# A block of mLSTM and sparse attention on one core: 256 bytes between two families of tiles, and the bias rows stored once

## The chip, the cores and the metric

The kernel runs on one core of one Trainium2 chip. The metric is device time in microseconds; less is better. The core has TensorE (matmuls), VectorE, ScalarE, POOL (GpSimd) and SP (SyncE); SP and POOL issue the transfers, which share 16 DMA engines.

## The reference

One layer on 256 tokens of width 4096, all in float32:

```
h = rmsnorm(x) * norm_w
u = h @ w_in                       # 4096 x 15424, split into 16 parts
y_ml = mlstm(conv/silu(q, k), v, gates), normed per head, * sigmoid(o) * silu(z)
y_ns = nsa(q, compressed, selected and window keys/values, rel_bias) * silu(z)
x = x + concat(y_ml, y_ns) @ w_out               # 4096 x 4096
x = x + sigmoid(x @ ple_gate) * (p @ ple_proj)   # 4096 x 4096, 256 x 4096
```

In `nsa` each score gets a bias that depends on the head and, through 32 buckets, on the distance of query and key: `bias = rel_bias[bucket(t - s)]`, with s > t masked. With 256 tokens all blocks are selected and the window holds all of them, so that selected and window branch differ in their keys and values only.

## The kernel before, in words

**The wide matmuls.** A float32 product is made of three float32r products. An operand `a` is split into `a_hi`, its rounded copy, and `a_lo = a - a_hi`; the result is `hi*hi + hi*lo + lo*hi`. The activations are the stationary operands: 8 tiles `sh0` to `sh7` (high parts) and 8 `sl0` to `sl7` (low parts), each 128 partitions x 4 x 256, 4096 bytes in a partition, filled for the first phase by `split_x` and for the later two by `t_stat`. The weights stream as the moving operand: a unit is a 512 KB block of 256 rows x 512 columns, loaded by SP into one of five `raw` buffers, split by ScalarE (`whi`, line 983) and VectorE (`wlo`, line 984) into one of three buffers each, two units ahead (`LOOK = 2`), and used in 12 matmuls (`mm` in `wide_group`, lines 725 to 735): for each of two row blocks j, `whi` with `sh` for both token halves t, `whi` with `sl` for both, `wlo` with `sh` for both. 16 units make a group of 512 output columns. There are 30 groups for `w_in`, 8 for `w_out` and 8 for `ple_gate`, and between them units of other kinds: 4 for the small columns of `w_in` (`small_group`, where the roles of weights and activations are exchanged), 16 for the compression and 8 for `ple_proj` (`proj_unit`, lines 885 to 897, with the stationary tiles `ph` and `pl`).

**Order.** The program's order is written out: the main loop at the end of `hymba_block` issues for each unit the split of the unit two ahead, the next load, the unit's matmuls, and then one `step()` of a queue of generators that hold all other work (`t_nq`, `t_mlstm` and so on). Each engine works in that order.

**The bias.** `t_tables` makes the row `p0[head, i]` by a matmul of the table with a one-hot matrix (`_onehot`), copies it to `rext` (16 x 384) and stores it to `rext_d` in device memory, 128 copies for each head (line 189). In `t_nq`, once for each of four head groups, `load_tb(h)` fetches for each head a tile `tb` of 128 x 256 (line 407): partition p reads 256 values from the p-th copy, shifted by p, so that row p of `tb` holds the bias of query p against keys in rising order. `bias_max` adds it to the scores in PSUM (line 471), for both branches at once. `tb` has three buffers, shared with `mb` of the mLSTM, whose 128 partitions all read the same 1 KB row of `mrow_d` (`load_m`, line 574).

**Where tiles lie.** A pool places its tags one behind another in the order in which they are first used, each tag with all its buffers. In the pool `wk` that order is `u` (3 buffers), `raw` (5 x 4096 bytes in a partition), `whi` and `wlo` (3 x 4096 each), then `sh0`, `sl0`, `sh1`, `sl1` and so on, among them `nat0` to `nat3` (8192 each; they also hold `kh` and `kl`), then `qt` (2 x 4096; `qh` and `ql`), `s` (3 x 2048), `sq` (4096), `b` (8320; also `vsw` and `pl`), `pt` (2 x 2048), `tb` (3 x 1024) and `a` (8320; also `ph`). So before the change `raw`, `whi`, `wlo`, all `sh` and `sl`, `nat`, `qt` and `b` start at the same place within 512 bytes, and `a` 128 bytes further on (8320 is 16 x 512 + 128).

Of the kernel before, what the change touches and what calls it, by code (L numbers as in the profile page):

```python
# [11 lines left out]
F32 = mybir.dt.float32  # L12
# [32 lines left out]
def hymba_block(ctx: ExitStack, tc: tile.TileContext, a, out: bass.AP):  # L45
    nc = tc.nc
# [5 lines left out]
    wk = ctx.enter_context(tc.tile_pool(name="work", bufs=1))  # L52
    psp = ctx.enter_context(tc.tile_pool(name="psum", bufs=1, space=bass.MemoryType.PSUM))
    drp = ctx.enter_context(tc.tile_pool(name="dram", bufs=1, space=bass.MemoryType.DRAM))
    ctx.enter_context(tc.manual_schedule())

    def side(i, shape):
        return psp.tile(shape, F32, tag=f"sd{i}", name=f"sd{i}")
# [4 lines left out]
    def sqtile(shape):  # L63
        return wk.tile(shape, F32, tag="sq", name="sq")

    def stile(shape):
        return wk.tile(shape, F32, tag="s", name="s", bufs=3)
# [4 lines left out]
    def small(shape, tag, bufs=2):  # L72
        return sm_.tile(shape, F32, tag=tag, name=tag, bufs=bufs)
# [47 lines left out]
    hss = cp.tile([128, 2, 8], F32, name="hss")  # L121
    rr = cp.tile([128, 2, 8], F32, name="rr")
    mrow_d = drp.tile([8, 256], F32, name="mrow_d")
    rext_d = drp.tile([16, 128, 384], F32, name="rext_d")


    fifo, urgent = deque(), deque()
# [45 lines left out]
    def t_tables():  # L173
        oh = sqtile([33, 864])
        nc.gpsimd.dma_start(oh, a["onehot"])
        for _ in range(4):
            yield
        p0 = side(0, [16, 384])
        MM(p0, rel33, oh[:, 0:384], start=True, stop=True)
        p1 = side(1, [128, 15, 16])  # L180
        for c in range(15):

            i0 = 384 + 128 - 16 * c - 31 + 255
            MM(p1[:, c, :], oh[:, i0:i0 + 128], rel33, start=True, stop=True)
            if c % 5 == 4:
                yield
        rext = stile([16, 384])
        nc.vector.tensor_copy(rext, p0)
        nc.gpsimd.dma_start(rext_d, rext[:, None, :].to_broadcast([16, 128, 384]))
        nc.vector.tensor_copy(biasc[:, 0:15], p1)  # L190
        yield

# [195 lines left out]
    def t_nq(flag, g):  # L388
# [14 lines left out]
        tb = {}  # L403

        def load_tb(h):
            tb[h] = wk.tile([128, 256], F32, tag="tb", name="tb", bufs=3)
            nc.gpsimd.dma_start(tb[h], bass.AP(tensor=rext_d.tensor,  # L407
                                               offset=rext_d.offset + (4 * g + h) * 128 * 384 + 127,
                                               ap=[[383, 128], [1, 256]]))

        for h in range(2):
            load_tb(h)
# [42 lines left out]
        def scores(i):  # L455
            h, t = units[i]
            n = 128 * (t + 1)
            psd[i] = side(0, [128, 2, n])
            r = slice(t * 128, (t + 1) * 128)
            MM(psd[i], qh[:, h, r], kh[:, g, :, 0:n], start=True, stop=False)  # L460
            MM(psd[i], ql[:, h, r], kh[:, g, :, 0:n], start=False, stop=False)  # L461
            MM(psd[i], qh[:, h, r], kl[:, g, :, 0:n], start=False, stop=True)  # L462
            if t == 0 and h + 2 < 4:
                load_tb(h + 2)

        def bias_max(i):
            h, t = units[i]
            n = 128 * (t + 1)
            sb[i] = stile([128, 2, n])
            bias = tb[h] if t else tb[h][:, 128:256]  # L470
            nc.vector.tensor_tensor(sb[i], psd[i], bias[:, None, :].to_broadcast([128, 2, n]), op=OP.add)  # L471
            mx[i] = small([128, 2], "mx2", 3)
            nc.vector.tensor_reduce(mx[i], sb[i], axis=AX.X, op=OP.max, negate=True)  # L473
# [41 lines left out]
        for i in range(11):  # L515
            at(scores, i)
            at(scale, i - 2)
            at(expo, i - 1)
            at(copy_pt, i - 3)
            yield  # L520
            at(coef, i - 1)
            at(bias_max, i)
            at(trans, i - 2)
            at(pv, i - 3)
            yield
# [123 lines left out]
    sh, sl = [None] * 8, [None] * 8  # L649

    def new_stat(c):
        sh[c] = wk.tile([128, 4, 256], F32R, tag=f"sh{c}", name=f"sh{c}")
        sl[c] = wk.tile([128, 4, 256], F32R, tag=f"sl{c}", name=f"sl{c}")

# [98 lines left out]
    def add(*gens):  # L753
        fifo.extend(gens)
# [4 lines left out]
    def split_x(k):  # L759
        c, kk = divmod(k, 4)  # L760
        if kk == 0:
            new_stat(c)
        x = xraw[c][:, kk]
        nc.scalar.activation(sh[c][:, kk], x, AF.Copy, scale=nw[:, k:k + 1])  # L764
        nc.vector.scalar_tensor_tensor(sl[c][:, kk], x, nw[:, k:k + 1], sh[c][:, kk],  # L765
                                       op0=OP.mult, op1=OP.subtract)

    def p1_post(name):
# [3 lines left out]
        def post(ps, flag):  # L772
# [4 lines left out]
            elif name in ("ks", "kw"):  # L777
                add(t_k(ps, flag, int(name == "kw")))
                if name == "kw":
                    add(t_tables())  # L780
            elif name in ("vs", "vw"):
                add(t_v(ps, flag, int(name == "vw")))
            elif kind == "nz":
                urgent.append(t_nz(ps, flag, i))
            elif kind == "nq":
                urgent.append(t_evac(ps, flag))
                add(t_nq(flag, i))
            elif kind in ("mq", "mk"):
                urgent.append(t_evac(ps, flag))
                add(t_mqk(flag, int(kind == "mk"), i))  # L790
            elif kind == "mv":
                urgent.append(t_mv(ps, flag, i))
                if i == 3:
                    add(t_mlstm(1))
            elif kind == "mz":
                add(t_mz(ps, flag, i))
                if i == 1:
                    add(t_mlstm(0))
            elif kind == "mo":
                add(t_mo(ps, flag, i))  # L800
                ch = [(c, (c * 512 + 2048) % 4096, f"p1_{c}", f"y{c}") for c in range(8)]
                if i == 2:
                    add(t_stat(ch[:7], range(16)))
                if i == 3:
                    add(t_stat(ch[7:], range(16)))
# [81 lines left out]
    def proj_unit(n):  # L887
        def mm(hi, lo):
            ps = [side(2 * (n % 2) + t, [128, 512]) for t in range(2)]
            ph, pl = held["ph"], held["pl"]  # L890
            for t in range(2):
                tk = slice(t * 128, (t + 1) * 128)
                for j in range(2):
                    MM(ps[t], ph[:, j, tk], hi[:, j, :], start=(j == 0), stop=False)  # L894
                    MM(ps[t], pl[:, j, tk], hi[:, j, :], start=False, stop=False)  # L895
                    MM(ps[t], ph[:, j, tk], lo[:, j, :], start=False, stop=(j == 1))  # L896
            pbox[n] = ps
        gemm_unit(a["ple_proj"][n], mm, (lambda: require("r7")) if n == 0 else None)
# [12 lines left out]
    def t_out(ps, flag, n):  # L911
        u = utile([128, 2, 512])
        if n == 7:
            for t in range(2):
                for c in (slice(0, 256), slice(256, 512)):
                    nc.scalar.activation(u[:, t, c], ps[t][:, c], AF.Sigmoid)
                    nc.vector.tensor_tensor(u[:, t, c], u[:, t, c], pbox[n][t][:, c], op=OP.mult)
                    nc.vector.tensor_add(u[:, t, c], u[:, t, c], nat[3][:, t, 512 + c.start:512 + c.stop])
                nc.sync.dma_start(out[t * 128:(t + 1) * 128, n * 512:(n + 1) * 512], u[:, t])
            done.add(flag)  # L920
            return
        for t in range(2):
            nc.scalar.activation(u[:, t], ps[t], AF.Sigmoid)
        done.add(flag)
        yield
        for t in range(2):
            nc.vector.tensor_tensor(u[:, t], u[:, t], pbox[n][t], op=OP.mult)
            nc.vector.tensor_add(u[:, t], u[:, t], nat[n // 2][:, t, (n % 2) * 512:(n % 2) * 512 + 512])
            nc.gpsimd.dma_start(out[t * 128:(t + 1) * 128, n * 512:(n + 1) * 512], u[:, t])
            yield  # L930

    for n in range(8):
        wide_group(f"g{n}", a["ple_gate"][n], "r" if n == 0 else None,
                   lambda ps, flag, n=n: add(t_out(ps, flag, n)), after=lambda u, n=n: proj_unit(n) if u == 7 else None)
# [86 lines left out]
def _bucket(dist):  # L1021
    n = np.maximum(dist, 0)
    nf = np.maximum(n, 1).astype(np.float32)
    large = 16 + (np.log(nf / np.float32(16)) / np.float32(np.log(8.0)) * np.float32(16)).astype(np.int32)
    return np.where(n < 16, n, np.minimum(large, 31))


def _onehot():
    d = np.concatenate([255 - np.arange(384), np.arange(480) - 255])
    o = np.zeros((33, d.size), np.float32)  # L1030
    o[np.where(d < 0, 32, _bucket(d)), np.arange(d.size)] = 1.0
    return o
# [63 lines left out]
```

## Time and profile before

| | |
|---|---|
| Median of 3 runs | 2208.91 us (2208.33 to 2209.18) |
| Profiled execution | 2208.36 us, its span 2206.6 us |
| Mean granted TensorE clock | 0.998 of full |
| TensorE busy | 2190.5 us, 99% of the span |
| VectorE, ScalarE busy | 1155.1 and 993.9 us, 52% and 45% |
| Moved by DMA | 425.14 MB, mean 193 GB/s |

The span goes from the first to the last instruction; the profiled execution's time holds 1.76 us around it. Busy times are unions of an engine's instructions; a matmul's recorded end is modelled, since matmuls overlap in the engine, so that the distance of starts tells the pace. Idle time of an engine that is not the bottleneck costs nothing.

### The profile page before, as it was taken

The numbers are of one execution on the slowest core, as the hardware profiler recorded it, in microseconds if no ns is written. First come the engines' busy times: TensorE is split into PE (matmuls) and PEld (weight loads), VectorE is DVE, ScalarE is ACT, GpSimd is POOL, SyncE is SP. The second block draws the span as 40 slices with busy tenths as digits, with TensorE's granted clock in tenths as the row PEclk, the third lists the DMA queues.
The fourth block names the chain that finished last, engine by engine and source line by source line (L and its number), as shares of the span: only waits on it lengthen the run. The fifth ranks groups of instructions, "written<-read, shape, count | busy, mean of one in ns | idle before, by whom it ended". The sixth has DMA issues, their size and how long they took to land.

```text
span 2206.6 us, 26113 instructions
## 1 busy us (share of the span) xinstructions
PE 2190.5 (99%) x10020; PEld 1800.3 (82%) x10020; DVE 1155.1 (52%) x1361; ACT 993.9 (45%) x1235; POOL 38.7 (2%) x82
## 2 busy tenths in 40 slices
PE   9999998999999999999999999999999999999998
PEld 7876886888888888888888888888888888888887
DVE  6553553555555565744574445564444455544544
ACT  6543443454545455444454344453333344444443
POOL 1000000000000000000000000000000000000000
PEclk9999999999999999999999999999999999999999
DMA  9667568655545454665556665656666655666664
GB/s 356 206 199 262 187 191 174 206 170 165 167 158 179 155 171 147 181 199 185 179 188 196 195 185 175 205 188 206 203 210 205 196 175 186 203 211 201 204 204 134
DMA packets 118796, 425.14 MB, mean 193 GB/s; under 512 B 13794, under 2 KB 13834, under 8 KB 118672
## 3 DMA queue, kind: packets, MB, share of 16 engines
q1 hardware_dynamic: 113840, 408.47, 58.3%
q0 software_dynamic: 4688, 15.00, 3.0%
q8 instruction: 78, 1.28, 0.2%
q14 instruction: 46, 0.38, 0.0%
q10 hardware_dynamic: 144, 0.02, 0.0%
HBM read 416.08 MB, written 7.35 MB: 192 GB/s over the span
## 4 chain that ended last, share of the span: by engine, by line
PE 98%; DMA 1%; DVE 0%; ACT 0%; SPq 0%; issue 0%; ACTq 0%
PE mm L733 60%; PE mm L735 30%; DMA raw<-in_w_in 1%; PE sd L508 1%; PE sd L843 1%; PE sd L663 1%; PE sd L504 1%; PE sd L495 0%; PE sd L203 0%; PE sd L894 0%; PE sd L896 0%; PE sd L895 0%; PE sd L418 0%; PE sd L462 0%; PE sd L461 0%; PE sd L460 0%
## 5 line engine op out<-in xcount | busy, mean ns | idle before, releaser
L984 DVE TENSOR_TENSOR wlo<-raw,whi 128x1024 fp32r<-128x1024 f32 x743 | 910.3, 1225 | 990.0 <-ACT whi L983 981.1
L983 ACT ACTIVATE whi<-raw 128x1024 fp32r<-128x1024 f32 x743 | 787.5, 1060 | 1108.0 <-PE mm L733 986.5
L733 PE MATMUL mm<-whi,sh 128*128 128x512 f32 x2940 | 920.0, 394 | 7.6 <-ACT whi L983 7.6
L733 PE MATMUL mm<-whi,sl 128*128 128x512 f32 x2940 | 908.4, 390 | 0.0
L735 PE MATMUL mm<-wlo,sh 128*128 128x512 f32 x2940 | 907.6, 390 | 0.2
L735 PEld LDWEIGHTS mm<-wlo,sh 128*128 128x128 f32 x2940 | 552.4, 188 | 117.4 <-DVE wlo L984 1.5
L733 PEld LDWEIGHTS mm<-whi,sl 128*128 128x128 f32 x2940 | 552.7, 188 | 116.6
L733 PEld LDWEIGHTS mm<-whi,sh 128*128 128x128 f32 x2940 | 543.7, 188 | 121.2 <-ACT whi L983 10.5
L508 PE MATMUL sd<-vsw,pt 128*128 128x128 f32 x192 | 29.9, 292 | 0.0
L478 ACT ACTIVATE s<-s,mx 128x128 f32<-128x128 f32 (+1 forms) x64 | 28.2, 442 | 0.4 <-DVE mx L473 0.4
L508 PEld LDWEIGHTS sd<-vsw,pt 128*128 128x128 f32 x192 | 23.8, 191 | 3.9
L488 ACT ACTIVATE s<-s,sm 128x128 f32<-128x128 f32 (+1 forms) x64 | 25.2, 441 | 0.4 <-DVE sm L484 0.3
L547 DVE SCALAR_TENSOR_TENSOR sq<-u,convw_c,sq 128x256 f32<-128x256 f32 x48 | 23.3, 485 | 1.7
L152 ACT ACTIVATE u<-mm,rt 128x512 f32<-128x512 f32 x12 | 8.2, 687 | 25.4 <-PE mm L735 25.4
L473 DVE TENSOR_REDUCE mx<-s 128x2 f32<-128x256 f32 (+1 forms) x32 | 17.7, 553 | 1.1
L471 DVE TENSOR_TENSOR s<-sd,tb 128x256 f32<-128x256 f32 (+1 forms) x32 | 17.7, 553 | 0.0
L500 DVE COPY pt<-sd 128x256 f32<-128x256 f32 (+1 forms) x32 | 17.6, 551 | 0.0
L843 PE MATMUL sd<-raw,xq 128*60 128x256 f32 x128 | 17.3, 391 | 0.0
L407 POOL DMA_DIRECT2D tb<-rext_d x16 | 8.6, 537 | 469.4 <-DVE s L471 405.4
L154 DVE TENSOR_SCALAR u<-mm,rt 128x512 f32<-128x512 f32 x12 | 9.0, 751 | 14.5 <-PE mm L735 14.5
L495 PEld LDWEIGHTS sd<-idn,s 128*128 128x128 f32 x96 | 12.4, 140 | 4.2
L765 DVE SCALAR_TENSOR_TENSOR sl<-u,nw,sh 128x256 fp32r<-128x256 f32 x32 | 14.1, 481 | 3.1 <-ACT sh L764 3.0
(223 smaller groups left out, 704.0 us busy)
## 6 DMA issues: line engine op xcount, KB each, us to landing
raw<-in_w_in SPq DMA_DIRECT2D x479, 512.0 KB, 3.5
raw<-in_w_out SPq DMA_DIRECT2D x128, 512.0 KB, 3.5
raw<-in_ple_gate SPq DMA_DIRECT2D x128, 512.0 KB, 4.1
raw<-in_w SPq DMA_DIRECT2D x16, 512.0 KB, 3.5
u<-in_xt SPq DMA_DIRECT2D x16, 256.0 KB, 7.8
xn<-in_x SPq DMA_DIRECT2D x4, 1024.0 KB, 6.7
u<-in_x POOLq DMA_DIRECT2D x8, 512.0 KB, 4.2
raw<-in_ple_proj SPq DMA_DIRECT2D x8, 512.0 KB, 3.8
```

The lines of the kernel that those rows point to most:

```text
L471: nc.vector.tensor_tensor(sb[i], psd[i], bias[:, None, :].to_broadcast([128, 2, n]), op=OP.add)
L478: nc.scalar.activation(sb[i][:, b], sb[i][:, b], AF.Exp, bias=mx[i][:, b:b + 1], accum_out=sums[i][:, b:b + 1])
L488: nc.scalar.activation(sb[i][:, b], sb[i][:, b], AF.Copy, scale=sums[i][:, b:b + 1])
L504: MM(o[t][:, h, :], pct[32 * h:32 * h + NCMP, t, :], vcmp[32 * h:32 * h + NCMP, g, :], start=True, stop=False)
L508: MM(o[t][:, h, :], ptb[i][:, b, s, :], v[:, s, b, g * 128:(g + 1) * 128], start=False, stop=(b == 1 and s == t))
L547: nc.vector.scalar_tensor_tensor(acc[:, h], c[:, h, i:i + 256], w[:, i:i + 1], acc[:, h], op0=OP.mult, op1=OP.add)
L663: nc.tensor.transpose(pp[i // 2][:, i % 2, t * 128:(t + 1) * 128], src[:, t, k:k + 128], idn)
L733: MM(box["ps"][t], s[c][:, k, t * 128:(t + 1) * 128], m[:, j, :], start=st, stop=False)
L735: MM(box["ps"][t], sh[c][:, k, t * 128:(t + 1) * 128], lo[:, j, :], start=False, stop=last)
L843: MM(o[64 * kv:64 * kv + 60], xq[l // 8][:, l % 8, 60 * kv:60 * kv + 60], raw[:, j, 256 * kv:256 * kv + 256], start=(l == 0), stop=(l == 31))
L983: nc.scalar.activation(hi, r, AF.Copy)
L984: nc.vector.tensor_sub(lo, r, hi)
```

## The change

Two things are changed that do not touch each other.

First, a tile `gap` of 128 x 64 float32 (256 bytes in a partition), which nothing writes or reads, is asked for just before `sh0`. All tags that come behind it in the pool `wk` start 256 bytes later; `u`, `raw`, `whi` and `wlo` stay where they were.

Second, the bias row is stored once for each head (16 x 384 in place of 16 x 128 x 384), and in rising order of distance. Partition p of `tb` then reads the 256 values that start at p + 1 of that one row, which puts the keys in falling order, and `bias_max` reads the tile backwards.

```diff
@@ hymba_block
-    rext_d = drp.tile([16, 128, 384], F32, name="rext_d")
+    rext_d = drp.tile([16, 384], F32, name="rext_d")
@@ t_tables
         nc.vector.tensor_copy(rext, p0)
-        nc.gpsimd.dma_start(rext_d, rext[:, None, :].to_broadcast([16, 128, 384]))
+        nc.gpsimd.dma_start(rext_d, rext)
@@ load_tb
             nc.gpsimd.dma_start(tb[h], bass.AP(tensor=rext_d.tensor,
-                                               offset=rext_d.offset + (4 * g + h) * 128 * 384 + 127,
-                                               ap=[[383, 128], [1, 256]]))
+                                               offset=rext_d.offset + (4 * g + h) * 384 + 1,
+                                               ap=[[1, 128], [1, 256]]))
@@ bias_max
-            bias = tb[h] if t else tb[h][:, 128:256]
+            bias = tb[h][:, n - 1::-1] if n == 256 else tb[h][:, 127::-1]
@@ new_stat
     def new_stat(c):
+        if c == 0 and sh[0] is None:
+            wk.tile([128, 64], F32, name="gap")
         sh[c] = wk.tile([128, 4, 256], F32R, tag=f"sh{c}", name=f"sh{c}")
         sl[c] = wk.tile([128, 4, 256], F32R, tag=f"sl{c}", name=f"sl{c}")
@@ _onehot
-    d = np.concatenate([255 - np.arange(384), np.arange(480) - 255])
+    d = np.concatenate([np.arange(384) - 128, np.arange(480) - 255])
```

## Rows read from the trace of the kernel before

**Rows 1.** The page's busy us of each engine, share of the span, instructions.

```profile
PE 2190.5 (99%) x10020; PEld 1800.3 (82%) x10020; DVE 1155.1 (52%) x1361; ACT 993.9 (45%) x1235; POOL 38.7 (2%) x82
```

**Rows 2.** From the page, the chain that ended last, by engine and by line.

```profile
PE 98%; DMA 1%; DVE 0%; ACT 0%; SPq 0%; issue 0%; ACTq 0%
PE mm L733 60%; PE mm L735 30%; DMA raw<-in_w_in 1%; PE sd L508 1%; PE sd L843 1%; PE sd L663 1%; PE sd L504 1%; PE sd L495 0%; PE sd L203 0%; PE sd L894 0%; PE sd L896 0%; PE sd L895 0%; PE sd L418 0%; PE sd L462 0%; PE sd L461 0%; PE sd L460 0%
```

**Rows 3.** The page's groups: busy us, mean ns of one, idle before.

```profile
L735 PE MATMUL mm<-wlo,sh 128*128 128x512 f32 x2940 | 907.6, 390 | 0.2
```

**Rows 4.** Timeline of TensorE, 1600 to 1611 us: start, us, instruction, count.

```profile
1601.14 0.62 PE L733 MATMUL mm<-whi,sh 128*128 128x512 f32 x2
...
1610.66 0.62 PE L733 MATMUL mm<-whi,sh 128*128 128x512 f32 x2
```

**Rows 5.** DMA issues: queue, count, KB each, median us to landing.

```profile
rext_d<-s POOLq DMA_DIRECT2D x1, 3072.0 KB, 35.4
tb<-rext_d POOLq DMA_DIRECT2D x16, 128.0 KB, 3.3
...
mb<-mrow_d POOLq DMA_DIRECT2D x8, 128.0 KB, 4.9
```

**Rows 6.** Timeline of POOL, 340 to 390 us, idle time before.

```profile
381.95 1.08 POOL L407 DMA_DIRECT2D tb<-rext_d  x2 [34.60 <-DMA rext_d<-s]
```

**Rows 7.** Stretch, length; busy PE, PEld, DVE, ACT, POOL; clock, DMA share, GB/s.

```profile
355.00:366.70 11.70, 11.70 (x53) 9.49 (x51) 3.68 (x3) 2.40 (x3) 0.00 (x0) 1.00 0.97 119
...
372.40:379.30 6.90, 5.49 (x12) 3.81 (x12) 1.23 (x1) 1.06 (x2) 0.00 (x0) 0.59 1.00 177
379.30:386.50 7.20, 6.47 (x24) 4.39 (x25) 4.34 (x4) 3.44 (x5) 1.86 (x4) 1.00 1.00 382
```

**Rows 8.** Timeline of 366 to 387 us, TensorE and ScalarE.

```profile
366.24 0.61 PE L735 MATMUL mm<-wlo,sh 128*128 128x512 f32 x2
371.35 1.06 ACT L983 ACTIVATE whi<-raw 128x1024 fp32r<-128x1024 f32 x1 [12.01 <-DMA raw<-in_w_in]
...
372.46 1.22 PE L733 MATMUL mm<-whi,sh 128*128 128x512 f32 x2 [5.61 <-ACT whi L983]
...
386.51 0.61 PE L733 MATMUL mm<-whi,sh 128*128 128x512 f32 x2
```

**Rows 9.** Instructions that touch tb: ns min/median/max, first and last start.

```profile
L471 DVE TENSOR_TENSOR s<-sd,tb x32: 417/554/687, 448.6 to 866.2; 128x256 f32<-128x256 f32 x16, 128x512 f32<-128x512 f32 x16
```

**Rows 10.** Groups by shape, line 471 on VectorE: busy us, mean ns.

```profile
L471 DVE TENSOR_TENSOR s<-sd,tb 128x512 f32<-128x512 f32 x16 | 10.9, 684 | 0.0
L471 DVE TENSOR_TENSOR s<-sd,tb 128x256 f32<-128x256 f32 x16 | 6.8, 423 | 0.0
```

**Rows 11.** Busy us of each engine in the first attention group's stretch.

```profile
420.00:540.00 120.00, 120.00 (x578) 98.97 (x578) 66.59 (x97) 60.80 (x98) 2.46 (x5) 1.00 0.54 167
```

**Rows 12.** Line 735, ns min/median/max: 366.7-372 us, then 1600-1700.

```profile
L735 PE MATMUL mm<-wlo,sh x1: 388/388/388, 366.5 to 366.5; 128*128 128x512 f32 x1
...
L735 PE MATMUL mm<-wlo,sh x147: 388/389/390, 1600.7 to 1700.0; 128*128 128x512 f32 x147
```

**Rows 13.** Timeline of TensorE about the first projection unit, 1851 to 1855 us.

```profile
1851.73 0.40 PE L894 MATMUL sd<-whi,ph 128*128 128x512 f32 x1
...
1854.54 0.63 PE L733 MATMUL mm<-whi,sh 128*128 128x512 f32 x2
```

**Rows 14.** Line 895 over the span: ns min/median/max.

```profile
L895 PE MATMUL sd<-whi,pl x32: 393/397/398, 1852.0 to 2178.6; 128*128 128x512 f32 x32
```

**Rows 15.** Timeline of TensorE about a score, 452 to 454 us.

```profile
452.46 0.39 PE L460 MATMUL sd<-kh,qh 128*128 128x512 f32 x1
...
453.14 0.62 PE L733 MATMUL mm<-whi,sh 128*128 128x512 f32 x2
```

**Rows 16.** Timeline of TensorE in the mLSTM, 1031 to 1033 us.

```profile
1031.23 0.60 PE L601 MATMUL sd<-mv,pt 128*128 128x257 f32 x2
...
1032.10 0.60 PE L603 MATMUL sd<-mv,pt 128*128 128x257 f32 x2
```

## The prediction

> **What bounds the kernel now.** I read the page's first line of engines, then the chain that ended last, then the groups of instructions, and only then single stretches. TensorE is busy for 2190.5 of 2206.6 us, VectorE and ScalarE for about half [rows 1], and the chain is TensorE for 98%, 90% of it the three-product matmuls of lines 733 and 735 [rows 2]. So two things can change the time: the pace of those matmuls, and the places where TensorE stands still. There are 46 wide groups of 16 units of 12 matmuls, 8832 in all (the groups show 2940 of each of three kinds [rows 3]; 12 more, the last unit's, are written out at line 722). Their pace is read from starts, since ends are modelled: from 1601.14 to 1610.66 us lie 42 matmuls, 226.7 ns each, 2.72 us a unit [rows 4]. 512 columns at the 2.4 GHz level are 213.3 ns, so 13.3 ns of each matmul is something else. The one item in the chain that is not TensorE is a weight load from memory, 1% [rows 2]; it is a single stop, and the change reaches it.
>
> **The stop at 367 us.** The DMA list has one large entry that is no weight: the copy of the bias rows, 3072 KB, 35.4 us to landing [rows 5]. The first tb load on POOL waits for it for 34.60 us and goes out at 381.95 [rows 6], so it ran from about 346. Between 355 and 379 us the 16 DMA engines are full, yet move 119 to 177 GB/s; about its landing they move 382 [rows 7]. The weight loads share these engines, and the ring of five raw tiles runs dry. The last pair of a unit starts at 366.24, so the next unit was due at 366.69; it starts at 372.46, two more follow late, and the fourth starts at 386.51 [rows 8]. ScalarE's split ahead of it had waited 12.01 us for raw, not for TensorE [rows 8], so the data was late. Part of the loss is the clock: TensorE stood still, and in the stretch from 372.40 the granted clock is 0.59 of full, so mostly the 1.2 GHz level [rows 7]. In all, 386.51 - 366.69 = 19.82 us for three units that take 8.16: 11.66 us lost, after which the pace is the old one.
>
> **The change, part by part.**
>
> *The row copy.* 3072 KB become 24 KB (16 rows of 1.5 KB), still one DMA on POOL's queue. The stop goes if its cause goes; bounds are 0 (another cause) and 11.66 us. I take 11.66, because the DMA engines are full in just this stretch and before it the loads kept up. POOL's wait of 34.60 us for the landing [rows 6] shrinks to a few us; behind it on POOL stand the tb loads and the clearing of sc, and nothing else late waits for those: the first tb load went out at 381.95 and is first read at 448.6 [rows 6, 9].
>
> *The tb loads.* As before 16 loads of 128 KB, but the 128 partitions now read overlapping stretches of the same 1.5 KB. The nearest row is mb, where all partitions read one 1 KB row: 4.9 us against 3.3 [rows 5]. So 0 to 1.6 us more for each, 25.6 us of transfer at most. Hidden: two loads are issued at a head-group's start, and the rest when heads 0 and 1 are done with a buffer, two heads ahead of their use; in 448.6 to 866.2 us 16 heads are worked [rows 9], so some 26 us for each. Without that cover it would be 1.6 us times 16 on the path.
>
> *The reversed read.* 32 additions on VectorE, 684 and 423 ns at the two shapes [rows 10], now step backwards through tb. No row shows such a read. Bounds: no difference, or doubled, 16 x (0.684 + 0.423) = 17.7 us in all. I take none: the nearest rows are these instructions themselves, and shapes, types and the PSUM operand stay as they are. Its cover: VectorE is busy for 66.6 of 120 us in a head-group's stretch [rows 11], and 4.4 us more for its four heads fit beside that; with the cover gone it would be the 17.7 us.
>
> *The gap.* It lies behind whi and wlo, so the split weights stay where they are and every sh and sl tile moves by 256 bytes. Tags lie in order of first use, and all these tiles are 4096 bytes (or 8192), with slices at multiples of 512. So before, every stationary slice has the same place within 512 bytes as the moving tile beside it; after, it is 256 bytes off. What is this worth? TensorE loads the next stationary slice while the present matmul streams. One matmul had no load beside it, the last before the stop, because the next load waited for the split: 388 ns, against a median of 389 with a load beside it [rows 12]. It is one sample of a modelled end, but the matmuls that are slow by their starts are long by this measure too (below). So in step, the load costs 1 to 2 ns, and the 13.3 ns is nearly all the matmul's own and out of the gap's reach. Bounds: the group mean of 390 ns for a kind without waits [rows 3], less 388, times 8832, is 17.7 us of gain at most. On the other side stand the projection's matmuls. Their stationary tiles ph and pl lie in tags a and b, and ph is 128 bytes off whi within 512, pl is not: 12 of them take from 1851.73 to 1854.54, 234.2 ns each, and the median is 397 instead of 389 [rows 13, 14]. That is 7.5 ns worse, times 8832 = 66 us. The scores, whose tiles moved with each other and lie at one place within 512, hold the old pace right after wide matmuls: three from 452.46 to 453.14 [rows 15], 226.7 ns each. I take 0 between -17.7 and +66: in the projection the offset changes from one matmul to the next, while behind the gap it is one and the same for all, as it is now.
>
> The Trainium skill, in "SBUF — State Buffer", section "Who interferes with whom", gives TensorE two independent read ports, one for the moving operand and one for weight loads. By that rule an address could not matter and the gap is worth 0. The projection's row, at 234.2 ns, disagrees with it; the matmul without a load, at 388 ns, nearly agrees.
>
> *Sum.* The profiled execution took 2208.36 us, its span 2206.6 and 1.76 around it. 2208.36 - 11.66 + 0 + 0 = 2196.70. The median of the runs lies 0.55 above the profiled one, so 2197.2; I forecast **2197 us**, 0.53% faster.
>
> **Rivals.**
>
> *The gap takes away what the load still costs.* For: that cost is seen, 1 to 2 ns [rows 3, 12]. Against: an offset of 256 bytes stands in no row. Time: 2197 less 0 to 17.7, so 2179 to 2195, the middle 2188.
>
> *Slower: the gap puts the loads out of step.* The mechanism is the projection's, in all 8832 matmuls. It decides from 11.66 us / 8832 = 1.3 ns per matmul; the full price gives 2263. For: the only row with another offset is slower. Against: it is a mixture of offsets.
>
> *The 13.3 ns are a collision after all, and the gap takes it away.* Matmuls that read at half the rate (257 columns in the time of 512) carry little: four from 1031.23 to 1032.10, 217.5 ns each, against 214.2 for their columns [rows 16], an excess of 3.3. If the wide ones came down to this, 10 ns x 8832 = 88 us: 2109. Against it speaks the 388 ns of the matmul with nothing beside it. The Trainium skill, "TensorE: Matmul & The Clock Gate", section "Wait — 56ns, not 53.3ns?", gives 2.5 ns of fixed cost per matmul and 215.7 ns for 512 columns; by that the wide matmuls have some 11 ns to lose, 97 us, an estimate from that page. The trace's 226.7 ns disagrees with it for this data type.
>
> *The stop stays.* If 128 partitions that read one row hold up the weight loads, or the stop has another cause, the time is 2208. Against: eight mb loads do the same, and the chain names no stop there [rows 2, 5].
>
> **How the numbers follow.** Forecast as summed 0.50; the load's cost goes 0.25; out of step 0.15; the collision 0.04; the stop stays 0.06. The first two and the stop that stays lie in 2179 to 2212 and hold 0.81; upwards that includes a loss of 1.7 ns per matmul on top of the stop's gain. The forecast's own range is 2193 to 2200. About 0.2%, 4.4 us, is what a measurement of this kernel can tell from no change. Faster by more: 0.50 + 0.25 + 0.04 and a little of the stop that stays, 0.81. Slower by more: 0.14 of the out of step case. The rest, 0.05, within.
>
> **What would show it.** Right: the chain has no weight load of 25 us, TensorE is busy throughout 355 to 395 us, rext_d is 24 KB and lands in a few us; line 471 stays at 684 and 423 ns; tb lands in 3 to 5 us; starts of wide matmuls stay 226.7 ns apart, median 389. Wrong: starts 225 apart or less (the first rival), 228 or more (the second), 217 (the third), or ScalarE waiting for raw about 370 us (the last).

## The result, and the profile after

The changed kernel takes 2197.34 us (median of 4 runs, 2196.65 to 2197.64), the kernel before 2208.62 us on the same chip (4 runs, 2207.94 to 2209.18): a ratio of 0.9949, 95% interval 0.9931 to 0.9966. The forecast was 2197 us. The profiled execution took 2197.64 us, its span 2195.9. One run of e9_shift below took 3590.20 us at a granted clock of 0.571, and its figures are those of the other three.

The page of the changed kernel: busy us of each engine with share and instructions, and the chain that ended last.

```profile
PE 2187.6 (100%) x10020; PEld 1799.3 (82%) x10020; DVE 1154.4 (53%) x1361; ACT 994.0 (45%) x1235; POOL 38.2 (2%) x82
...
PE 100%; DVE 0%; ACT 0%; ACTq 0%; issue 0%
```

Beside [rows 1, 2] the chain has lost its only item of 1% or more that was not TensorE, the weight load. The groups of matmuls (busy us, mean ns of one, idle before) have not moved by more than 1 ns; the third row answers to [rows 3]. Two line numbers more come from the lines of the gap.

```profile
L735 PE MATMUL mm<-whi,sh 128*128 128x512 f32 x2940 | 918.8, 394 | 0.0
L735 PE MATMUL mm<-whi,sl 128*128 128x512 f32 x2940 | 906.6, 390 | 0.0
L737 PE MATMUL mm<-wlo,sh 128*128 128x512 f32 x2940 | 905.8, 389 | 0.0
```

The stretches about the old stop, with the columns of [rows 7]:

```profile
355.00:366.70 11.70, 11.70 (x53) 9.71 (x52) 5.79 (x5) 5.52 (x6) 0.00 (x0) 1.00 0.67 200
366.70:372.40 5.70, 5.70 (x27) 4.73 (x26) 2.71 (x3) 2.12 (x2) 0.00 (x0) 1.00 0.67 215
372.40:379.30 6.90, 6.90 (x32) 5.69 (x32) 2.52 (x3) 3.11 (x3) 0.00 (x0) 1.00 0.60 178
379.30:395.00 15.70, 15.70 (x71) 13.01 (x70) 7.35 (x6) 5.75 (x7) 0.00 (x0) 1.00 0.59 195
```

TensorE is busy throughout, the clock is at its upper level, and up to 379 us the DMA engines are at 0.60 to 0.67 instead of full, while they move 178 to 215 GB/s instead of 119 to 177. The timeline of POOL (idle time before, and what ended it), then the issues of DMA (KB each, median us to landing), show why:

```profile
347.30 0.52 POOL L189 DMA_DIRECT2D rext_d<-s  x1 [35.56 <-DVE s L188]
350.53 1.10 POOL L407 DMA_DIRECT2D tb<-rext_d  x2 [2.72 <-DMA rext_d<-s]
```

```profile
tb<-rext_d POOLq DMA_DIRECT2D x16, 128.0 KB, 4.1
mb<-mrow_d POOLq DMA_DIRECT2D x8, 128.0 KB, 4.9
rext_d<-s POOLq DMA_DIRECT2D x1, 24.0 KB, 2.9
```

The first `tb` load waits 2.72 us for the row copy instead of 34.60 [rows 6]. Last, the timeline of TensorE far behind (start, us, instruction, count), where 24 matmuls lie between the first two rows, 226.7 ns each, as in [rows 4], and near the end:

```profile
1600.45 0.62 PE L735 MATMUL mm<-whi,sl 128*128 128x512 f32 x2
...
1605.89 0.62 PE L735 MATMUL mm<-whi,sl 128*128 128x512 f32 x2
...
2185.65 0.61 PE L737 MATMUL mm<-wlo,sh 128*128 128x512 f32 x2
```

Both traces hold 10,020 matmuls in the same order, so they can be laid on each other by number. Of the following rows the first two are of before, the third of after:

```profile
320.35 0.62 PE L735 MATMUL mm<-wlo,sh 128*128 128x512 f32 x2
2196.32 0.62 PE L735 MATMUL mm<-wlo,sh 128*128 128x512 f32 x2
321.35 0.61 PE L737 MATMUL mm<-wlo,sh 128*128 128x512 f32 x2
```

The matmul that starts at 320.35 us before starts at 321.35 after, 1.00 us later; the one at 2196.32 before is the last row of the fence above, 2185.65, 10.67 us earlier. Matched so at every 500th matmul, the difference is the same on either side of the stretch from 367 to 387 us, within 0.01. The whole gain is 10.67 + 1.00 = 11.67 us and lies in that stretch. The 1.00 us was lost in the first 13 us (the first wide matmul starts at 7.22 instead of 6.61 and runs longer); over the kernels below that start-up comes out from 0.12 us earlier to 1.00 later, with and without the change.

### The profile page after: what moved, and what is told of

It is laid out like the page before. It is cut to its first block, busy times and chain, and to the rows that moved or that the text cites. A ratio compares the mean times of both kernels' runs of the same rounds, so it can differ in the third digit from the quotient of the medians.

```text
span 2195.9 us, 26113 instructions
## 1 busy us (share of the span) xinstructions
PE 2187.6 (100%) x10020; PEld 1799.3 (82%) x10020; DVE 1154.4 (53%) x1361; ACT 994.0 (45%) x1235; POOL 38.2 (2%) x82
## 4 chain that ended last, share of the span: by engine, by line
PE 100%; DVE 0%; ACT 0%; ACTq 0%; issue 0%
PE mm L735 61%; PE mm L737 30%; PE sd L508 1%; PE sd L845 1%; PE sd L665 1%; PE sd L504 1%; PE sd L495 0%; PE sd L203 0%; PE sd L896 0%; PE sd L897 0%; PE sd L898 0%; PE sd L418 0%; PE sd L462 0%; PE sd L461 0%; PE sd L90 0%; PE sd L460 0%
## 5 line engine op out<-in xcount | busy, mean ns | idle before, releaser
L495 PE MATMUL sd<-idn,s 128*128 128x128 f32 x96 | 15.6, 272 | 0.0
```

The costliest lines, as they stand in the source:

```text
L495: nc.tensor.transpose(psd[i][:, b, s, :], sb[i][:, b, s * 128:(s + 1) * 128], idn)
```

## The experiments

All differences below are to the changed kernel unless it is said otherwise; the kernel before took 2208.43 us beside e1 to e4, 2209.14 beside e5 to e8, 2208.48 beside e9 and e10, and 2209.83 in its one run beside e11 and e12.

### One half of the change alone

**e1_rows:** the changed kernel without the gap.

```diff
-        if c == 0 and sh[0] is None:
-            wk.tile([128, 64], F32, name="gap")
```

> The changed kernel without the gap: only the bias rows stored once and read backwards. If the stop at 367 us was the whole of the change (my sum), this gives the changed kernel's time, 2197.3 us, 0.995 of before, with starts of wide matmuls 226.7 ns apart. If instead the gap gave part of the 11.3 us (the rival in which it takes away what the weight load costs), this lies between 2198 and 2208 us, by as much as the gap gave.

2197.2 us (2197.03 to 2197.7), 0.995 of before, interval 0.9933 to 0.9966.

**e2_gap:** the kernel before with the gap alone.

> The kernel before with the gap of 256 bytes alone. My sum: no difference, 2208.6 us, starts 226.7 ns apart, the stop of 11.7 us still there. If the gap takes away what the load costs: up to 17.7 us less. If it puts loads out of step in part, some us more.

2208.67 us in 10 runs, 1.0001 of before, interval 0.9992 to 1.001. The stop is there as it was; the timeline of TensorE in e2_gap:

```profile
366.58 0.61 PE L737 MATMUL mm<-wlo,sh 128*128 128x512 f32 x2
372.38 1.22 PE L735 MATMUL mm<-whi,sh 128*128 128x512 f32 x2 [5.18 <-ACT whi L985]
```

So the row copy is the whole gain, and a gap of 256 bytes is worth nothing.

### Is a constant distance harmless?

The prediction gave the gap 0 because the distance between moving and stationary tiles is the same for all matmuls. Three kernels change only its size.

**e3_gap128:** 128 bytes.

```diff
-            wk.tile([128, 64], F32, name="gap")
+            wk.tile([128, 32], F32, name="gap")
```

> The changed kernel with a gap of 128 bytes in place of 256, so that the stationary tiles lie 128 bytes off the moving ones, as ph does in the projection. If the projection's slow matmuls come from this offset, and 256 bytes were harmless only because they repeat some period, all wide matmuls now start 234 ns apart instead of 226.7 and the time is about 2197 + 66 = 2263 us. If addresses play no part (the rule of two independent read ports), 2197 us and 226.7 ns.

2243.91 us, 1.0161 of before, interval 1.0145 to 1.0176: slower by 46.6 us. Between these rows of its timeline lie 48 matmuls, 232.1 ns each:

```profile
1600.67 0.62 PE L735 MATMUL mm<-whi,sh 128*128 128x512 f32 x2
...
1611.81 0.64 PE L735 MATMUL mm<-whi,sh 128*128 128x512 f32 x2
```

5.4 ns times 8832 is 47.7 us, which covers it; it is less than the 234 ns and the 66 us that the projection's price gave. A constant distance can cost.

**e5_gap64** (`[128, 16]`) and **e6_gap384** (`[128, 96]`), 64 and 384 bytes.

> The changed kernel with a gap of 64 bytes. The gap of 128 bytes cost 46.6 us. If only an offset of a multiple of 256 keeps TensorE in step, 64 bytes cost tens of us as well: 2217 to 2263 us, starts 229 to 234 ns apart. If 128 bytes are a special case, 2197 us and 226.7 ns.

> The changed kernel with a gap of 384 = 256 + 128 bytes. If the place within 256 bytes is all that counts, this is the kernel with the gap of 128 again: 2244 us, starts 232 ns apart. If 256 bytes helped or 128 hurt for another reason (the place within 512 bytes, or where the tiles lie as such), another time, between 2197 and 2263.

64 bytes: 2251.5 us, 1.0194 of before, interval 1.0179 to 1.0209, slower by 54.2 us. 384 bytes: 2244.31 us, 1.016, interval 1.0145 to 1.0176, slower by 47.0 us, as with 128. Of e5_gap64, 48 matmuls of 233.3 ns:

```profile
1599.69 0.63 PE L735 MATMUL mm<-whi,sh 128*128 128x512 f32 x2
...
1610.89 0.63 PE L735 MATMUL mm<-whi,sh 128*128 128x512 f32 x2
```

With 0 and 256 bytes alike, and 128 and 384 alike, the five sizes fit a period of 256 bytes; what it is in the chip that repeats, no run here shows.

**e9_shift:** is it the distance, or the place of one of the tiles? Here a pad ahead of all work tiles grows by 64 bytes, so that moving and stationary tiles move together.

```diff
-    sm_.tile([128, 16], F32, name="pad")
+    sm_.tile([128, 32], F32, name="pad")
```

> The changed kernel with the pad ahead of the work tiles twice as wide: all of them, moving and stationary, lie 64 bytes further, and the distance between any two of them stays what it was. Theory (the pace of a matmul goes by the distance of its two operands within 256 bytes): nothing changes, 2197 us, 12 matmuls of the projection's partner L737 in 2.72 us, 226.7 ns each. Rival (it goes by the place of the stationary tile alone, or of the moving tile alone, within 256 bytes): a shift of 64 bytes costs about what the gap of 64 bytes cost, some 40 to 55 us, so 2240 to 2255 us, and 230 ns or more a matmul.

2197.52 us (2197.3 to 2198.04, three runs), 0.9951 of before, interval 0.9934 to 0.9967. 24 matmuls lie between these rows of its timeline, 226.7 ns each:

```profile
1601.14 0.62 PE L735 MATMUL mm<-whi,sh 128*128 128x512 f32 x2
...
1606.58 0.62 PE L735 MATMUL mm<-whi,sh 128*128 128x512 f32 x2
```

64 bytes between the two families cost 54 us, 64 bytes under both of them nothing: it is the distance. Nor do ScalarE and VectorE make it, which fill the moving tiles meanwhile: by the trace of e3, from 1400 to 1500 us, the wide matmuls take 232.3 ns beside ScalarE alone, 232.5 beside VectorE alone and 232.4 beside neither.

**e4_ph:** if so, the projection's 234.2 ns [rows 13] come from `ph` alone, which lies 128 bytes off. A pad of 128 bytes ahead of its tag brings it to the place of the others.

```diff
+        if j == 0:
+            wk.tile([128, 32], F32, name="gap2")
```

> The changed kernel with 128 further bytes ahead of the tag a, so that ph lies at the same place within 512 bytes as the split weights, and no tile lies at an odd multiple of 128 off them. If the offset makes the projection slow, its 96 matmuls now start 226.7 ns apart; the time falls by 0.7 us, too little to measure, so the rows decide. If addresses play no part, they stay at 234 ns.

2196.71 us in one run. The timeline of e4_ph about the first projection unit, 12 matmuls in 2.72 us, 226.7 ns each:

```profile
1841.07 0.39 PE L898 MATMUL sd<-whi,ph 128*128 128x512 f32 x1
...
1843.79 0.62 PE L737 MATMUL mm<-whi,sh 128*128 128x512 f32 x2
```

The slow projection is gone. e4 takes away the 128 bytes and, within 256 bytes, also the "mixture of offsets", so it is e3 that tells them apart: there a constant 128 bytes is slow without any mixture. The mixture costs more all the same, 7.5 ns against 5.4; why, is open.

The one run is 0.63 us below the median of the changed kernel, too little to tell; but by number its trace gains 0.12 us on the changed kernel's at each of the eight units, 0.95 in all, and more than the 96 x 7.5 ns = 0.72 us of their own matmuls. The wide matmuls right behind a unit are slow too: in the changed kernel six of them lie between these rows, 231.7 ns each.

```profile
1843.88 0.63 PE L735 MATMUL mm<-whi,sh 128*128 128x512 f32 x2
...
1845.27 0.62 PE L735 MATMUL mm<-whi,sh 128*128 128x512 f32 x2
```

So the price is not a matmul's alone; it carries over to its neighbours. The scores of e3 show the same. Their two tiles moved together, as [rows 15] have them at 226.7 ns, yet three matmuls of a score take 0.70 us there, and 228 to 236 ns each over the sixteen such scores:

```profile
480.86 0.40 PE L460 MATMUL sd<-kh,qh 128*128 128x512 f32 x1
...
481.56 0.62 PE L735 MATMUL mm<-whi,sh 128*128 128x512 f32 x2
```

### What of the matmul's 226.7 ns can be had

**e10_bf16:** the split operands in 2 bytes.

```diff
-F32R = mybir.dt.float32r
+F32R = mybir.dt.bfloat16
```

> The changed kernel with the split operands kept in bfloat16 instead of the rounded 4-byte type, with tiles of half the bytes; the products are coarser by it. The same matmuls in number and columns. Theory (226.7 ns is a price of the 4-byte operands, as the same kernel's 217.5 ns of L601 and L603 for 2-byte ones suggests): about 216 ns a matmul of 512 columns, 11 ns less on some 9,000 of them, so 2090 to 2110 us. Rival (226.7 ns comes from the order of matmuls and weight loads, whatever the type): 2190 to 2200 us.

2091.67 us (2091.6 to 2093.03), 0.9471 of before, interval 0.9455 to 0.9487. In the timeline of e10_bf16, 60 matmuls lie between these rows, 215.7 ns each, 11.0 less; in the groups (mean ns) a weight load has halved, from 188:

```profile
1599.79 0.59 PE L735 MATMUL mm<-whi,sl 128*128 128x512 bf16 x2
...
1612.73 0.59 PE L735 MATMUL mm<-whi,sl 128*128 128x512 bf16 x2
```

```profile
L737 PEld LDWEIGHTS <-sh 128*128 128x128 bf16 x2940 | 287.7, 98 | 347.7 <-issue 0.9
```

11.0 ns x 8832 are 97 of the 105.7 us. By the traces the other matmuls of split operands give some 3.4 us more; the last 5 us were not traced. Since moving operand and weight load shrink together, e10 does not say which of the two took the 11 ns. Its expectation came out partly by luck: the 217.5 ns that it leans on are of float32 matmuls of 257 columns [rows 16], not of 2-byte ones.

**e11_half_load** and **e12_half_gap128** ask that: 14 of 16 units of each group load and use only 64 of the 128 columns of the stationary slice, so that half of the outputs lose these contributions.

```diff
+                    e = 64 if 0 < u < 15 else 128
...
-                            MM(box["ps"][t], s[c][:, k, t * 128:(t + 1) * 128], m[:, j, :], start=st, stop=False)
+                            MM(box["ps"][t][0:e], s[c][:, k, t * 128:t * 128 + e], m[:, j, :], start=st, stop=False)
```

> The changed kernel in which 14 of the 16 units of a wide group load and multiply only 64 of each stationary slice's 128 columns (half of the outputs lose these contributions); the moving side stays at 512 columns. So each of their weight loads is halved and the number of matmuls is the same. Theory (at a distance of 0 or 256 bytes the pace is the matmul's own, for 4-byte operands): still 226.7 ns each, about 2197 us. Rival (the 13.3 ns over the 213.3 of 512 columns are what the load takes from the matmul beside it): 6 to 7 ns less on 7728 matmuls, 220 ns each and about 2147 us.

> The same with a gap of 128 bytes, which cost 46.6 us with whole loads (about 232.1 ns a matmul where the gap of 256 had 226.7). Theory (what an unfavourable distance costs is a meeting of the load's reads with the matmul's reads, so it goes with the length of the load): half of it, 229 to 230 ns and 2217 to 2223 us, if the units with half loads had 226.7 at the gap of 256. Rival (the matmul pays by its own place, whatever the load): 232 ns, 2244 us.

e11: 2217.48 us in one run, slower by 20.1, which neither theory had. e12: 2221.82 us in one run. The timelines, first of e11 (18 matmuls with half loads, then 24 with whole ones), then of e12 (36 with half loads):

```profile
1600.07 0.63 PE L738 MATMUL mm<-wlo,sh 128*64 128x512 f32 x2
...
1604.21 0.63 PE L738 MATMUL mm<-wlo,sh 128*64 128x512 f32 x2
1604.68 0.61 PE L736 MATMUL mm<-whi,sh 128*128 128x512 f32 x2
...
1610.12 0.63 PE L736 MATMUL mm<-whi,sh 128*64 128x512 f32 x2
```

```profile
1600.08 0.63 PE L738 MATMUL mm<-wlo,sh 128*64 128x512 f32 x2
...
1608.33 0.63 PE L738 MATMUL mm<-wlo,sh 128*64 128x512 f32 x2
```

In these stretches a matmul with half loads takes 230.0 ns at a distance of 256 bytes and 229.2 at 128; with whole loads it is 226.7 and 232.1. The groups of e11 have the half load at 134 ns (mean) where the whole one takes 188, so it is shorter, but not by half, and the matmul uses half the columns too. So here a shorter load made no matmul cheaper, and with it the distance hardly matters. The time of e12 falls into what the theory of the load's length gave, but the condition it set, 226.7 ns in e11, did not hold; it does not count for it. Why a half load costs 3.3 ns where a whole one at the right distance does not, stays open, and so does why the whole kernel lost 20.1 us and not 3.3 ns x 7728 = 25.5.

### What made the stop

**e7_half:** the changed kernel, and on POOL's queue ahead of the row copy a write that nobody reads, with half the bytes of the old one: 16 partitions, 64 copies of 1.5 KB each.

```diff
+    more_d = drp.tile([16, 64, 384], F32, name="more_d")
...
+        nc.gpsimd.dma_start(more_d, rext[:, None, :].to_broadcast([16, 64, 384]))
```

> The changed kernel that also writes 64 copies of each bias row, 1536 KB, to a place that nothing reads: half of what the kernel before wrote. The stop began 20 us after that write, when the ring of raw tiles was empty. If it is starvation with a threshold, half the write is over in some 18 us, before the ring is empty, and costs under 1 us: 2197 to 2198 us. If the loss goes with the bytes, it is half of 11.7 us: 2203.

2198.6 us (2197.74 to 2199.54), 0.9953 of before, interval 0.9937 to 0.997. The windows of e7_half, columns as in [rows 7], and its DMA issues:

```profile
355.00:366.70 11.70, 11.70 (x53) 9.70 (x52) 3.68 (x3) 2.74 (x3) 0.19 (x1) 1.00 0.94 172
366.70:372.40 5.70, 4.65 (x20) 3.19 (x19) 3.85 (x4) 4.25 (x4) 1.69 (x4) 1.00 0.98 379
```

```profile
more_d<-s POOLq DMA_DIRECT2D x1, 1536.0 KB, 19.1
rext_d<-s POOLq DMA_DIRECT2D x1, 24.0 KB, 18.8
```

Half the write takes 19.1 us, and TensorE stands still for 5.70 - 4.65 = 1.05 us; the time is 1.3 us above the changed kernel's where the whole write cost 11.66. That is above the 2197 to 2198 us expected of starvation with a threshold, but far from the 2203 of a loss that goes with the bytes: the first half of the write cost 1.3 us, the second some 10. The ring of raw tiles covers the loads' delay for about as long as the half write lasts.

**e8_wide:** as many bytes as the old write, 3072 KB, but from 128 partitions in rows of 6 KB.

```diff
+    more_d = drp.tile([128, 4, 1536], F32, name="more_d")
...
+        v = held["v"].rearrange("p a b c -> p (a b c)")[:, 0:1536]
+        nc.gpsimd.dma_start(more_d, v[:, None, :].to_broadcast([128, 4, 1536]))
```

> The changed kernel that also writes 3072 KB, as many bytes as before, but from a tile of 128 partitions in rows of 6 KB, to a place that nothing reads. If the bytes cause the stop, 2208 to 2209 us, the stop back. If it was the form of the write (2048 rows of 1.5 KB out of 16 partitions, 35.4 us), this one lands in some 15 us and costs nothing: 2197 to 2198.

2196.76 us (2196.54 to 2197.08), 0.9945 of before, interval 0.993 to 0.996. Its source was ready early, so POOL issued it at 310.60 us. The window from there to the landing, and the issue:

```profile
310.60:327.00 16.40, 16.40 (x78) 13.68 (x77) 9.20 (x11) 7.53 (x8) 0.79 (x2) 1.00 0.98 375
```

```profile
more_d<-vsw POOLq DMA_DIRECT2D x1, 3072.0 KB, 16.4
```

The engines are as full as in the stop, 0.98, but they move 375 GB/s, where the changed kernel moves 200 in the same window, so that the write rides on top of the weights and TensorE is busy throughout. It ran 36 us earlier than the old write, but the changed kernel moves the same 200 GB/s in either place. By the traces' lists of DMA packets, one of the old write, 4.6 KB, took 688 ns (median) and one of e8's, 6.1 KB, 234 ns. e8 changes the number of partitions and the length of the rows together, so which of the two held the engines is not shown.

## Why the prediction was right, and where its reasoning was not

**The stop: right, in place, price and cause.** The term was -11.66 us; the traces laid on each other give 11.67. Only the reason given for the cause, that "the DMA engines are full in just this stretch", is not enough: they were as full in e8 and nothing stopped. What stopped the loads was a write of 16 partitions in 1.5 KB rows that held the engines for 35.4 us [rows 5], at 119 to 177 GB/s in all [rows 7], longer than the five raw tiles last: TensorE stopped 20 us after its issue, and half of it, 19.1 us, cost only 1.3.

**The tb loads: right.** 4.1 us against 3.3, 0.8 more within the bounds of 0 to 1.6, and hidden: line 471, which reads them, has no idle time before it in the rows below.

**The reversed read: right.** Line 471 by shape in the changed kernel (busy us, mean ns), beside 684 and 423 ns in [rows 10]:

```profile
L471 DVE TENSOR_TENSOR s<-sd,tb 128x512 f32<-128x512 f32 x16 | 10.9, 682 | 0.0
L471 DVE TENSOR_TENSOR s<-sd,tb 128x256 f32<-128x256 f32 x16 | 6.7, 422 | 0.0
```

**The gap: the value 0 was right, the step to it wrong.** "In the projection the offset changes from one matmul to the next, while behind the gap it is one and the same for all, as it is now" takes constancy for what makes a distance harmless. e3, e5 and e6 have constant distances of 128, 64 and 384 bytes and lose 46.6, 54.2 and 47.0 us; e4 cures the projection by moving `ph` alone. 256 bytes cost nothing because, as the five sizes fit, the effect repeats after 256 bytes. No row of before showed that period: rows of distance 0 and one of 128 were all there was, so the 0.15 for the loads out of step was the right rival with a price in its range (46.6 us are 5.3 ns per matmul, where 7.5 was read from the projection), and with another gap it would have been the result. That 256 bytes were chosen, and not 128, is luck as far as the argument goes.

The Trainium skill's "SBUF — State Buffer", section "Who interferes with whom", gives TensorE two independent read ports, one for the moving operand and one for weight loads, and the prediction drew the same 0 from it. e3 disagrees with what was drawn: 128 bytes cost 46.6 us.

**The 13.3 ns: half right.** The prediction had it that "the load costs 1 to 2 ns, and the 13.3 ns is nearly all the matmul's own and out of the gap's reach". No gap took anything from 226.7 ns, and neither did a load of half the columns. But the pace is not out of the gap's reach upwards: a wrong distance adds 5.4 to 6.6 ns with whole loads, and half loads add 3.3. That a collision makes up the 13.3 ns had 0.04 and is not settled; what is shown is that most of it goes with the 4-byte operands, 11.0 of 13.3 ns in e10. There the Trainium skill's "TensorE: Matmul & The Clock Gate", section "Wait — 56ns, not 53.3ns?", 215.7 ns for 512 columns, is what the trace has, 215.7.

**Not in the sum:** the start-up, 1.00 us later in the profiled execution. Without it the profiled 2197.64 would have been 2196.6, against the sum of 2196.70.

## What to carry to other kernels

A copy that looks harmless in bytes can stop a kernel by its form, as this one did from 16 partitions in 1.5 KB rows: look at the GB/s beside the DMA share, and at how long it holds the engines against how long the loaded tiles last. When a change moves tiles, work out the distance of each matmul's two operands within 256 bytes before and after: here multiples of 256 kept the pace, and 64, 128 and 384 lost 2 to 2.5%. An argument that gives the right number from one other point of data deserves a second size, as 128 bytes did here.

## What the runs showed of the hardware

- The pace of a matmul of 512 columns with 4-byte operands goes by the distance of the moving and the stationary tiles: 226.7 ns at 0 and 256 bytes, 232.1 at 128, about 232 at 384, 233.3 at 64. Moving both by 64 bytes changes nothing. The loss carries over: six matmuls at a harmless distance right behind a projection unit took 231.7 ns each.
- Loading and using 64 of the 128 stationary columns made the matmuls slower, 230.0 ns in place of 226.7, with loads of 134 ns in place of 188.
- With 2-byte operands a matmul of 512 columns takes 215.7 ns, and the kernel 2091.67 us.
- 3072 KB written from 16 partitions in 1.5 KB rows took 35.4 us at the kernel's cost of 11.7; from 128 partitions in 6 KB rows 16.4 us, at no cost. The 24 KB behind the half write landed only with it, after 18.8 us.
- VectorE reading an operand backwards took 682 and 422 ns, forwards 684 and 423.
